# Norm chains ahead of weight parts, and sample products in larger steps, in a two-layer decoder step

## The chip, the cores and the metric

The kernel runs on one core of one Trainium2 chip. The metric is the device time of one execution in microseconds (us). An execution of the profiler gives the trace; the other times are without it. The engines are named as in the profile: PE (TensorE, the matrix products), PEld (its weight loads), DVE (VectorE), ACT (ScalarE), POOL (GpSimd), SP (SyncE, which here issues the loads).

## The reference

Two layers of a decoder trunk are computed for 256 prompt positions and 8 samples (one position each) that share the weights, 264 columns in all. Each layer adds four parts to x: half a SwiGLU feed-forward, a mixer (a short gated convolution in layer 0, the gated linear recurrence HGRN2 in layer 1), cross-attention to a memory, and half another SwiGLU.

```
def rmsnorm(x, g):
    y = xf * lax.rsqrt(jnp.mean(xf * xf, axis=-1, keepdims=True) + EPS)
    return (y * g.astype(jnp.float32)).astype(x.dtype)

def cross_attn(x, mk, mv, w_q, w_o):
    q = (x @ w_q).reshape(B, T, X_HEADS, X_HEAD_DIM)
    s = jnp.einsum('bthd,bnhd->bhtn', q, mk) / math.sqrt(X_HEAD_DIM)
    p = jax.nn.softmax(s, axis=-1)
    o = jnp.einsum('bhtn,bnhd->bthd', p, mv).reshape(B, T, D)
    return o @ w_o

        for i in range(DEPTH):
            h = rmsnorm(x, norm_ffn1[i])
            x = x + 0.5 * swiglu(h, w_ffn1_gate[i], w_ffn1_up[i], w_ffn1_down[i])
            h = rmsnorm(x, norm_mix[i])
            ...
            x = x + y
            h = rmsnorm(x, norm_xattn[i])
            x = x + cross_attn(h, mem_k[i], mem_v[i], w_xq[i], w_xo[i])
            h = rmsnorm(x, norm_ffn2[i])
            x = x + 0.5 * swiglu(h, w_ffn2_gate[i], w_ffn2_up[i], w_ffn2_down[i])
```

D is 1024, the feed-forward width 2816; attention has 4 heads of 256 and 256 memory positions, the recurrence 8 heads of 128. The prompt's memory keys and values are computed here (w_xkv, after a norm of the memory); the samples' keys and values (cache_mem_k, cache_mem_v, 8 MB each per layer) and the recurrence's states (8 x 8 matrices of 128 x 128) are read. All is float32.

## The kernel before, in words

**Products.** x stands transposed in memory: 8 tiles (KT) of 128 rows and 264 columns. Every float32 product of a projection is made of three fp32r products (mm3, L308 to L310): the high part of the activation times the high part of the weight, its low part times the weight's high part, and its high part times the weight's low part. kv (L847 to L849) does so with the memory as the stationary operand. Smaller things (transposes, scores, the samples' products) are plain f32 products, which leave two records each in the trace. Four PSUM banks take projections, four others ("aux") everything else.

**Weights.** Class Weights streams them in halves of 128 x 1024: SP loads raw, ACT casts it to wh (L107), DVE or, in attention's kv, POOL subtracts to wl (L119). Six buffers of raw, five of wh and wl.

**Norm chains.** A class Norm collects the squares of x, tile by tile, while the projection before it ends. Its finish() (L345 to L361) is a generator that runs beside the next projection: a cast nhi on ACT and nlo on DVE split the sums, two products with ones (ps_ms, L355 and L356) add over the rows, Ln and Exp on ACT (L288, helper rsqrt) and three Newton steps on DVE (L299, L303, L304) give R. The next projection runs on x without R; R enters where its banks are evicted (in attention qT, L833). So PE comes to wait for R only when it needs a fifth bank.

**What sets the order.** The program's lanes of generators (Flow) are advanced by a tick after every few products; each yield puts what follows one tick later. A scheduler then puts the instructions on the engines by that order and by priorities (tc.high_priority, offset HURRY), every engine runs its own in that order, and order() forbids it to put one instruction ahead of another on the same engine. One such bond exists: behind an out_proj the DVE parts wl stand behind the sum that frees a bank (L739).

**Attention.** mem_split (L819) makes mh and ml, eight high and low parts of the memory, on ACT and DVE. The query projection follows in four pieces; for each head sample_scores computes the samples' 64 dot products on DVE (L901) from a ring of four 1 MB slots. After it kv runs, head by head: its results become Kn and Vn (L857, ACT, then two output DMAs that ACT issues), transposed keys (pkt, L877; KTt), scores (psc, L929), softmax (mxp, Pp), transposed weights (ppt, L943; PTh, PTl) and values (po; oh, ol). The samples run beside: sample_rest takes maxima (mxs, transposed in pst, L976; top, tops, spread back by the product L980), exponentials, sums (L987), the weights Ps, and then the values spv (L1003), 128 rows from the ring by 8 columns, four heads side by side in 32 columns each; then os, spt and oh's sample columns (L1010 to L1018). Last comes the output projection.

**Recurrence.** samples() (L1237) multiplies the read states by the samples' queries (pqs, L1247), two heads and one ring slot at a time, in four columns of 32; head_norms (L1271) computes the norm of four heads (rr, rs), and gated (L1292) turns it into the output projection's input: prs (L1302), two products on DVE, then yh and yl, whose tiles are called kg and qf.

## Time and profile before

| | us |
|---|---|
| three runs, lowest / median / highest | 1303.28 / 1303.49 / 1303.51 |
| the profiled execution, whole | 1303.28 |
| its span, first to last instruction | 1301.3 |
| first attention: query projection's products | 301.6 to 327 |
| its kv, and its output projection | 327.2 to 393, 394.9 to 425 |
| recurrence: input projection, output projection | 809.3 to 942, 942.8 to 968 |
| second attention | 968.8 to 1091 |

The granted clock of PE was 0.997 of full speed. In the rows that follow, a line of the timeline gives start (us from the span's start), duration, engine, line of the kernel, operation, output <- inputs, shapes and count; brackets at its end tell how long the engine sat idle before it and for whom. "Duration" of a product includes its way through the array: back to back, products of one kind start 0.12 us apart (264 columns, fp32r) though each lasts 0.28. A row of the waits gives the engine, its line, whom it waited for, total us, times, and the longest.

### The profile page before, as it was taken

The numbers are of one execution on the slowest core, as the hardware profiler recorded it, in microseconds if no ns is written. First come the engines' busy times: TensorE is split into PE (matmuls) and PEld (weight loads), VectorE is DVE, ScalarE is ACT, GpSimd is POOL, SyncE is SP. The second block draws the span as 40 slices with busy tenths as digits, with TensorE's granted clock in tenths as the row PEclk, the third lists the DMA queues.
The fourth block names the chain that finished last, engine by engine and source line by source line (L and its number), as shares of the span: only waits on it lengthen the run. The fifth ranks groups of instructions, "written<-read, shape, count | busy, mean of one in ns | idle before, by whom it ended". The sixth has DMA issues, their size and how long they took to land.

```text
span 1301.3 us, 25953 instructions
## 1 busy us (share of the span) xinstructions
PE 1279.6 (98%) x10310; PEld 1236.4 (95%) x10310; DVE 824.1 (63%) x1570; ACT 694.5 (53%) x1146; POOL 293.5 (23%) x236
## 2 busy tenths in 40 slices
PE   8999999999999999999999999999999999999997
PEld 8999999999869999999999999999998779999996
DVE  6555567759826655556655545878789637766454
ACT  6454545446545645544554544656665447666542
POOL 3211231211741211132111132000023521211220
PEclk9999999999999999999999999999999999999998
DMA  8796555646997666556666556564557995776650
GB/s 269 245 302 178 166 182 175 208 142 201 357 379 218 195 180 178 185 164 201 179 178 186 176 175 186 157 195 136 169 157 257 394 327 160 223 215 198 204 167 34
DMA packets 263099, 266.75 MB, mean 205 GB/s; under 512 B 8697, under 2 KB 259577, under 8 KB 260930
## 3 DMA queue, kind: packets, MB, share of 16 engines
q1 hardware_dynamic: 257150, 259.78, 63.9%
q10 hardware_dynamic: 5828, 5.32, 1.2%
q8 instruction: 81, 1.33, 0.4%
q14 instruction: 40, 0.33, 0.1%
HBM read 255.00 MB, written 10.07 MB: 204 GB/s over the span
## 4 chain that ended last, share of the span: by engine, by line
PE 94%; DVE 3%; ACT 2%; issue 0%; DMA 0%; POOL 0%; DVEq 0%; SPq 0%; ACTq 0%; POOLq 0%
PE pj L308 20%; PE pj L309 19%; PE pj L310 19%; PE dn L308 7%; PE dn L310 7%; PE dn L309 7%; PE kv L847 2%; PE kv L849 2%; PE kv L848 2%; PE spv L1003 1%; PE psc L929 1%; PE pl L1163 1%; DVE wl L119 1%; PE pj L381 1%; DVE xl L332 1%; ACT wh L107 1%
## 5 line engine op out<-in xcount | busy, mean ns | idle before, releaser
L119 DVE TENSOR_TENSOR wl<-raw,wh 128x1024 fp32r<-128x1024 f32 (+1 forms) x347 | 426.6, 1234 | 248.8 <-ACT wh L107 238.0
L308 PE MATMUL pj<-xh,wh 128*128 128x264 f32 x1952 | 558.7, 286 | 2.3 <-DVE qT L833 2.3
L309 PE MATMUL pj<-xl,wh 128*128 128x264 f32 x1952 | 553.6, 284 | 0.0
L310 PE MATMUL pj<-xh,wl 128*128 128x264 f32 x1952 | 553.1, 283 | 0.0
L107 ACT CAST wh<-raw 128x1024 fp32r<-128x1024 f32 (+1 forms) x406 | 415.2, 1032 | 240.6 <-PE pj L309 108.3
L308 PEld LDWEIGHTS pj<-xh,wh 128*128 128x128 f32 x1952 | 367.8, 188 | 4.6 <-DVE qT L833 2.7
L309 PEld LDWEIGHTS pj<-xl,wh 128*128 128x128 f32 x1952 | 368.0, 189 | 0.0
L310 PEld LDWEIGHTS pj<-xh,wl 128*128 128x128 f32 x1952 | 366.2, 188 | 0.0
L308 PE MATMUL dn<-ah,wh 128*128 128x264 f32 x704 | 200.9, 285 | 0.0
L310 PE MATMUL dn<-ah,wl 128*128 128x264 f32 x704 | 200.0, 284 | 0.0
L309 PE MATMUL dn<-al,wh 128*128 128x264 f32 x704 | 199.4, 283 | 0.0
L119 POOL TENSOR_TENSOR wl<-raw,wh 128x1024 fp32r<-128x1024 f32 (+1 forms) x61 | 142.9, 2350 | 194.7 <-ACT wh L107 148.0
L703 POOL TENSOR_TENSOR al<-a,ah 128x264 fp32r<-128x264 f32 x88 | 90.1, 1026 | 415.6 <-ACT ah L702 415.5
L310 PEld LDWEIGHTS dn<-ah,wl 128*128 128x128 f32 x704 | 132.7, 188 | 0.0
L308 PEld LDWEIGHTS dn<-ah,wh 128*128 128x128 f32 x704 | 132.4, 188 | 0.2
L309 PEld LDWEIGHTS dn<-al,wh 128*128 128x128 f32 x704 | 132.5, 188 | 0.0
L288 ACT ACTIVATE g<-g 128x264 f32<-128x264 f32 x88 | 36.9, 424 | 78.9 <-DVE g L695 78.8
L702 ACT CAST ah<-a 128x264 fp32r<-128x264 f32 x88 | 36.0, 413 | 65.1 <-DVE a L701 64.3
L330 ACT ACTIVATE xh<-xT,gains 128x264 fp32r<-128x264 f32 x56 | 28.7, 513 | 75.9 <-DVE xT L729 59.2
L901 DVE CUSTOM_DVE_ANT_0 junk<-ring,pq 128x256 f32<-128x256 f32 x128 | 53.7, 420 | 3.7
L701 DVE TENSOR_TENSOR a<-g,pj 128x264 f32<-128x264 f32 x88 | 37.1, 426 | 29.0 <-PE pj L310 28.9
L695 DVE TENSOR_TENSOR g<-pj,R_norm_ffn 128x264 f32<-128x264 f32 x88 | 37.5, 429 | 28.1 <-PE pj L310 28.0
(329 smaller groups left out, 1494.3 us busy)
## 6 DMA issues: line engine op xcount, KB each, us to landing
raw<-in_w_ffn_gate_dram SPq DMA_DIRECT2D x88, 512.0 KB, 5.2
raw<-in_w_ffn_up_dram SPq DMA_DIRECT2D x88, 512.0 KB, 4.1
raw<-in_w_ffn_down_dram SPq DMA_DIRECT2D x64, 512.0 KB, 4.2
ring<-in_cache_mem_k_dram SPq DMA_DIRECT2D x16, 1024.0 KB, 6.6
raw<-in_w_xkv_dram SPq DMA_DIRECT2D x64, 256.0 KB, 3.6
ring<-in_cache_mem_v_dram SPq DMA_DIRECT2D x16, 1024.0 KB
raw<-in_w_rec_in_dram SPq DMA_DIRECT2D x32, 512.0 KB, 4.4
raw<-in_w_ffn_down_dram SPq DMA_DIRECT2D x32, 384.0 KB, 3.0
```

What stands on the lines that cost most here:

```text
L107: self.pin(copy(wh[:, :n], self.raw[i][:, :n]))
L119: ins = eng.tensor_sub(wl[:, :n], self.raw.pop(i)[:, :n], wh[:, :n].bitcast(F32))
L288: in_line(nc.scalar.activation(dst, src, func, **kw))
L308: nc.tensor.matmul(ps, wh[:, s], rh, start=first, stop=False)
L309: nc.tensor.matmul(ps, wh[:, s], rl, start=False, stop=False)
L310: nc.tensor.matmul(ps, wl[:, s], rh, start=False, stop=last)
L330: pin(nc.scalar.activation(h, src, AF.Copy, scale=g))
L695: nc.vector.tensor_mul(g, ps, norm.R)
L701: nc.vector.tensor_mul(a, g, ps)
L702: nc.scalar.copy(ah[:, blk], a)
L703: nc.gpsimd.tensor_sub(al[:, blk], a, ah[:, blk].bitcast(F32))
L901: nc.vector.tensor_tensor_reduce(junk, t[:, i % 8], pq[:, :XD], 1.0, 0.0, ALU.mult, ALU.add, sc[:, h, i : i + 1])
```

## The change

It does five things.

1. finish() of every norm loses one yield before the sums of squares, and Ln, Exp and the Newton steps get the priority HURRY. The last Exp and the last Newton step are noted in W.after; every later wh on ACT, wl on DVE, and the parts mh and ml are bound to stand behind them.
2. mem_split starts when the norm is done instead of after six ticks.
3. tops, the spread maxima, has 128 rows (zero below the fourth), and so has the product that uses it.
4. The values yield after two ring slots instead of one, and give both back together.
5. The recurrence's samples take four heads and two slots in one step, with one bank for its transposes and sums; the head norms and the gated products get HURRY and the same bond as in 1.

```diff
-        self.pin(copy(wh[:, :n], self.raw[i][:, :n]))
+        self.pin(self.behind(self.hi[i % len(self.hi)], copy(wh[:, :n], self.raw[i][:, :n])))
...
+    def behind(self, eng, ins):
+
+        if eng in self.after:
+            self.order(ins, self.after[eng], "products in line")
+        return ins
...
             yield
-            yield
             ps = aux_bank("ps_ms")
             nc.tensor.matmul(ps[:, :NC], ones_d, hi, start=True, stop=False)
             nc.tensor.matmul(ps[:, :NC], ones_d, lo, start=False, stop=True)
-            rsqrt(self.R, ps[:, :NC])
-            if self.after is not None:
-                use_set(self.after)
-            newton(self.R, ps[:, :NC], self.acc)
+            with tc.high_priority(offset=HURRY):
+                rsqrt(self.R, ps[:, :NC])
+                W.after["s"] = last[0]
+                if self.after is not None:
+                    use_set(self.after)
+                W.after["v"] = newton(self.R, ps[:, :NC], self.acc).ins
             self.done = True
...
             def mem_split():
-                for _ in range(6):
+                while not norm.done:
                     yield
                 for k in range(KT):
                     g = gcol("norm_mem", l, k)
-                    nc.scalar.activation(mh[:, k], memT[:, k], AF.Copy, scale=g)
...
+                    W.behind("s", nc.scalar.activation(mh[:, k], memT[:, k], AF.Copy, scale=g))
...
-                nc.tensor.matmul(pt[:, P : P + XH], tops, ident[:XH, :XH], start=True, stop=True)
+                nc.tensor.matmul(pt[:, P : P + XH], tops, ident[:, :XH], start=True, stop=True)
...
-                    if i % 2 == 1:
-                        ring.done((l, "v", i // 2))
+                    if i % 4 == 3:
+                        for i2 in (i // 2 - 1, i // 2):
+                            ring.done((l, "v", i2))
                         yield
...
             def samples(a):
 
                 s = gr[a]
-                for p in (2 * a, 2 * a + 1):
-                    hs = slice(2 * p, 2 * p + 2)
+                hs = slice(GH * a, GH * a + GH)
+                ps = aux_bank("pqs")
+                for p2 in range(2):
+                    p = 2 * a + p2
                     S0 = ring.tiles["s", p].rearrange("p (h b v) -> p h b v", h=2, b=NB)
-                    ps = aux_bank("pqs")
                     for j in range(4):
                         for c in range(4):
                             hh, hf = divmod(c, 2)
                             nc.tensor.matmul(
-                                ps[32 * c : 32 * c + 4, :P],
+                                ps[32 * c : 32 * c + 4, p2 * P : p2 * P + P],
...
-                    for c in range(4):
-                        nc.scalar.copy(os[32 * c : 32 * c + 4], ps[32 * c : 32 * c + 4, :P])
...
+                for c in range(4):
+                    nc.scalar.copy(os[32 * c : 32 * c + 4], ps[32 * c : 32 * c + 4, : 2 * P])
...
+                pd = pt[:, 2 * P : 2 * P + GH * NB]
+                nc.tensor.matmul(pd, ones_1, qk.rearrange("p a b -> p (a b)"), start=True, stop=True)
...
-                rsqrt(rr, pm[:, :NC])
-                use_set(SIGMOID)
-                newton(rr, pm[:, :NC], tmp)
-                nc.scalar.copy(rs, rr)
-                nc.vector.scalar_tensor_tensor(rs, rs.bitcast(F32), seconds_of, rr, op0=ALU.mult, op1=ALU.add)
+                with tc.high_priority(offset=HURRY):
+                    rsqrt(rr, pm[:, :NC])
+                    W.after["s"] = last[0]
+                    newton(rr, pm[:, :NC], tmp)
+                    nc.scalar.copy(rs, rr)
+                    use_set(SIGMOID)
+                    W.after["v"] = nc.vector.scalar_tensor_tensor(
+                        rs, rs.bitcast(F32), seconds_of, rr, op0=ALU.mult, op1=ALU.add
+                    ).ins
```

The three places at which the order matters most follow; names end in the scheduler's tile numbers, which differ between the two programs, and the new file's lines are 7 to 20 higher.

DVE in layer 0, from the split of the sum of squares (nlo) to the first evictions of the query projection (qT). Before:

```order
L351 TENSOR_TENSOR nlo<-nacc_norm_xattn_2596,nhi 128x264
L825 SCALAR_TENSOR_TENSOR ml<-memT,gains,mh 128x256 x8
L119 TENSOR_TENSOR wl_3905<-raw_3677,wh_3891 128x1024
L119 TENSOR_TENSOR wl_3932<-raw_3699,wh_3907 128x1024
L299 SCALAR_TENSOR_TENSOR nacc_norm_xattn_2596<-ps_ms,R_norm_xattn_2597 128x264
L303 SCALAR_TENSOR_TENSOR nacc_norm_xattn_2596<-nacc_norm_xattn_2596,R_norm_xattn_2597 128x264
L304 SCALAR_TENSOR_TENSOR R_norm_xattn_2597<-nacc_norm_xattn_2596,R_norm_xattn_2597 128x264
L833 TENSOR_TENSOR qT_3963<-pj_0_3825,R_norm_xattn_2597 128x264
L833 TENSOR_TENSOR qT_3963<-pj_1_3826,R_norm_xattn_2597 128x264
L833 TENSOR_TENSOR qT_3966<-pj_0_3827,R_norm_xattn_2597 128x264
```

After:

```order
L358 TENSOR_TENSOR nlo<-nacc_norm_xattn_2596,nhi 128x264
L306 SCALAR_TENSOR_TENSOR nacc_norm_xattn_2596<-ps_ms,R_norm_xattn_2597 128x264
L310 SCALAR_TENSOR_TENSOR nacc_norm_xattn_2596<-nacc_norm_xattn_2596,R_norm_xattn_2597 128x264
L311 SCALAR_TENSOR_TENSOR R_norm_xattn_2597<-nacc_norm_xattn_2596,R_norm_xattn_2597 128x264
L120 TENSOR_TENSOR wl_3915<-raw_3677,wh_3893 128x1024
L836 SCALAR_TENSOR_TENSOR ml<-memT,gains,mh 128x256
L120 TENSOR_TENSOR wl_3936<-raw_3699,wh_3917 128x1024
L845 TENSOR_TENSOR qT_3969<-pj_0_3827,R_norm_xattn_2597 128x264
L845 TENSOR_TENSOR qT_3969<-pj_1_3828,R_norm_xattn_2597 128x264
L845 TENSOR_TENSOR qT_3972<-pj_0_3829,R_norm_xattn_2597 128x264
L845 TENSOR_TENSOR qT_3972<-pj_1_3830,R_norm_xattn_2597 128x264
L836 SCALAR_TENSOR_TENSOR ml<-memT,gains,mh 128x256 x3
```

The three Newton steps (L306, L310, L311) now follow nlo at once; the eight ml, which stood ahead of them, are spread from there into the dot products, and two wl slid behind R.

ACT in layer 1, at the second head norm of the recurrence: from the table load ahead of Ln and Exp (rr) to the casts kg of the output projection's input. Before:

```order
L284 ACT_TABLE_LOAD
L288 ACTIVATE rr<-pm,eps_t 128x264
L107 CAST wh_11541<-raw_11209 128x1024
L288 ACTIVATE rr<-rr 128x264
L284 ACT_TABLE_LOAD
L107 CAST wh_11567<-raw_11241 128x1024
L288 ACTIVATE q<-G 128x264
L284 ACT_TABLE_LOAD
L1287 CAST rs<-rr 128x264
L107 CAST wh_11623<-raw_11331 128x1024
L107 CAST wh_11639<-raw_11375 128x1024
L1308 CAST kg<-oT 128x264 x4
```

After:

```order
L291 ACT_TABLE_LOAD
L295 ACTIVATE rr<-pm,eps_t 128x264
L295 ACTIVATE rr<-rr 128x264
L291 ACT_TABLE_LOAD
L295 ACTIVATE q<-G 128x264
L107 CAST wh_11516<-raw_11184 128x1024
L1303 CAST rs<-rr 128x264
L107 CAST wh_11542<-raw_11216 128x1024
L291 ACT_TABLE_LOAD
L1328 CAST kg<-oT 128x264
```

Ln and Exp stand side by side, two wh no longer stand between Ln and q, one follows q instead; a table load and a wh lie between rs and the first kg, where two wh stood.

PE in layer 0, at the end of kv. Before, the rows behind the last values (spv), and, after more kv products and the values po of head 2, the first rows of the output projection (pj of oh):

```order
L847 MATMUL kv_1_4721<-wh_4611,mh 128x512
L848 MATMUL kv_1_4721<-wl_4629,mh 128x512
L849 MATMUL kv_1_4721<-wh_4611,ml 128x512
L1014 MATMUL spt<-ident,os 128x128 x2
L943 MATMUL ppt<-ident,Pp 128x128 x4
L847 MATMUL kv_0_4720<-wh_4658,mh 128x512
```

```order
L308 MATMUL po<-PTh,Vh_4684 128x256
L309 MATMUL po<-PTl,Vh_4684 128x256
L310 MATMUL po<-PTh,Vl_4685 128x256
L308 MATMUL pj_0_4894<-oh,wh_4690 128x264
L309 MATMUL pj_0_4894<-ol,wh_4690 128x264
```

After, the rows behind the last values, up to the output projection's first:

```order
L1014 MATMUL spv<-ring_4642,Ps 8x256 x8
L860 MATMUL kv_0_4758<-wl_4733,mh 128x512
L861 MATMUL kv_0_4758<-wh_4691,ml 128x512
L859 MATMUL kv_1_4759<-wh_4691,mh 128x512
L860 MATMUL kv_1_4759<-wl_4733,mh 128x512
L861 MATMUL kv_1_4759<-wh_4691,ml 128x512
L1026 MATMUL spt<-ident,os 128x128 x2
L889 MATMUL pkt<-ident,Kn_4721 128x128 x4
L315 MATMUL pj_0_4895<-oh,wh_4735 128x264
L315 MATMUL pj_1_4896<-oh,wh_4735 128x264
L941 MATMUL psc<-KTt_4780,qT_4018 128x256 x4
L316 MATMUL pj_0_4895<-ol,wh_4735 128x264
```

The last values moved to five products ahead of kv's end; head 2's transposes (pkt, L889), scores (psc, L941) and all that follows now stand between or behind the first products of the output projection, which before had twelve po products ahead of it.

More of the change, by code (lines that the diff above doesn't have):

```diff
@@ L66, in __init__ @@
         self.pin = lambda ins: ins
-        self.behind = lambda ins: None
+        self.order, self.after = None, {}
     def add(self, *srcs):
@@ L274, in order @@
         tc.add_manual_dep(ins.ins, first.name, info, reason=reason)
+    W.order = order
     def in_line(ins):
@@ L303, in newton @@
         nc.vector.scalar_tensor_tensor(tmp, tmp, -0.5, dst, op0=ALU.mult, op1=ALU.mult)
[L304 removed]
+        return nc.vector.scalar_tensor_tensor(dst if out is None else out, tmp, 1.5, dst, op0=ALU.add, op1=ALU.mult)
     def mm3(ps, w, rh, rl, first, last, s=slice(None)):
@@ L404, in project @@
             W.release()
-            W.behind = lambda ins: None
             if need is not None:
@@ L738, in evac @@
             if k == KT - 1:
-                W.behind = lambda ins: order(ins, add.ins, "the sum that frees a bank")
+                W.after["v"] = add.ins
             nxt.kt(k)
@@ L817, in attention @@
             nc.gpsimd.memset(os, 0.0)
+            tops = ap.tile([P, P], F32, name="tops")
+            nc.gpsimd.memset(tops, 0.0)
             def mem_split():
-                for _ in range(6):
+                while not norm.done:
                     yield
@@ L971, in sample_rest @@
                 top = ap.tile([XH, NB], F32, name="top")
-                tops = ap.tile([XH, P], F32, name="tops")
                 nc.vector.reduce_max(mx, sc, axis=AX.X)
@@ L1035, in rec @@
             qfz = rp.tile([P, RH, 2, 16], F32, name="qfz")
-            os = rp.tile([P, P], F32, name="os")
+            os = rp.tile([P, 2 * P], F32, name="os")
             nc.gpsimd.memset(os, 0.0)
@@ L1253, in samples @@
                             )
-                    ring.done(("s", p))
-                    for c in range(4):
-                        nc.scalar.copy(os[32 * c : 32 * c + 4], ps[32 * c : 32 * c + 4, :P])
-                    qk = tl("qk", 2, (P, 2, NB))
-                    nc.vector.tensor_mul(qk, qs[:, hs], ks[:, hs])
-                    yield
-                    pt = aux_bank("pqt")
-                    nc.tensor.transpose(pt[:, :P], os, ident)
-                    pd = aux_bank("pd")[:, : 2 * NB]
-                    nc.tensor.matmul(pd, ones_1, qk.rearrange("p a b -> p (a b)"), start=True, stop=True)
-                    nc.vector.tensor_mul(oT[:, hs, T:], vs[:, hs], pd.rearrange("p (h b) -> p h b", h=2))
-                    dst = oT[:, hs, T:].rearrange("p h (f j) -> p h f j", f=2)
-                    ptv = pt[:, :P].rearrange("p (h f r) -> p h f r", h=2, f=2)[:, :, :, :4]
-                    nc.vector.tensor_add(dst, dst, ptv)
-                    yield
+                for p2 in range(2):
+                    ring.done(("s", 2 * a + p2))
+                for c in range(4):
+                    nc.scalar.copy(os[32 * c : 32 * c + 4], ps[32 * c : 32 * c + 4, : 2 * P])
+                qk = tl("qk", 1, (P, GH, NB))
+                nc.vector.tensor_mul(qk, qs[:, hs], ks[:, hs])
+                yield
+                pt = aux_bank("pqt")
+                for p2 in range(2):
+                    nc.tensor.transpose(pt[:, p2 * P : p2 * P + P], os[:, p2 * P : p2 * P + P], ident)
+                pd = pt[:, 2 * P : 2 * P + GH * NB]
+                nc.tensor.matmul(pd, ones_1, qk.rearrange("p a b -> p (a b)"), start=True, stop=True)
+                nc.vector.tensor_mul(oT[:, hs, T:], vs[:, hs], pd.rearrange("p (h b) -> p h b", h=GH))
+                dst = oT[:, hs, T:].rearrange("p h (f j) -> p h f j", f=2)
+                ptv = pt[:, : 2 * P].rearrange("p (h f r) -> p h f r", h=GH, f=2)[:, :, :, :4]
+                nc.vector.tensor_add(dst, dst, ptv)
+                yield
                 s["old"] = True
```

26 lines of the change are left out of this document (14 added, 12 removed).

## The prediction

> **What bounds the kernel now.** I read the page first (busy time by engine, then the chain of waits), then the table of PE's waits, then the timelines around each wait.
>
> ```profile
> PE 1279.6 (98%) x10310; PEld 1236.4 (95%) x10310; DVE 824.1 (63%) x1570; ACT 694.5 (53%) x1146; POOL 293.5 (23%) x236
> PE 94%; DVE 3%; ACT 2%; issue 0%; DMA 0%; POOL 0%; DVEq 0%; SPq 0%; ACTq 0%; POOLq 0%
> ```
>
> TensorE (PE) is the bound: busy 98% of the span, and 94% of the chain that ended last. The change alters almost none of its products, so only two things can move the time: microseconds in which PE stands, and what it pays to change from one kind of product to another. The table of PE's waits lists the first; its columns are total us, times, longest.
>
> ```profile
> PE pj L308 <- DVE qT L833: 2.3, 2, 1.2
> PE po L308 <- ACT PTh L949: 1.3, 2, 0.7
> PE pj L308 <- ACT oh L965: 1.3, 2, 0.7
> PE pj L308 <- ACT kg L1308: 1.3, 1, 1.3
> PE pst L980 <- DVE tops L978: 0.4, 2, 0.2
> ```
>
> Rows one and four are in reach of the change: 2.3 us at the query projections of both layers, 1.3 us at the output projection of the recurrence. Rows two and three are the last prompt head of each attention; its instructions keep their order, so they stay. No row names an evicted bank of a feed-forward part (g) or the conv part, so the norm chains of those stages hold PE up nowhere today.
>
> **A. Norm chain of attention (gain 2.35).** PE, DVE and ACT of layer 0:
>
> ```profile
> 309.04 0.28 PE L355 MATMUL ps_ms<-nhi,ones_d 128*128 128x264 f32 x1
> ...
> 313.40 0.29 PE L309 MATMUL pj<-xl,wh 128*128 128x264 f32 x1
> 313.53 0.28 PE L310 MATMUL pj<-xh,wl 128*128 128x264 f32 x1
> 315.04 0.39 PE L308 MATMUL pj<-xh,wh 128*128 128x264 f32 x1 [1.23 <-DVE qT L833]
> ...
> 307.30 0.42 DVE L351 TENSOR_TENSOR nlo<-nacc_norm_xattn,nhi 128x264 fp32r<-128x264 f32 x1
> 307.64 3.25 DVE L825 SCALAR_TENSOR_TENSOR ml<-memT,gains,mh 128x256 fp32r<-128x256 f32 x8
> 310.81 2.35 DVE L119 TENSOR_TENSOR wl<-raw,wh 128x1024 fp32r<-128x1024 f32 x2
> 313.08 0.43 DVE L299 SCALAR_TENSOR_TENSOR nacc_norm_xattn<-ps_ms,R_norm_xattn 128x264 f32<-128x264 f32 x1
> 314.55 1.46 DVE L833 TENSOR_TENSOR qT<-pj,R_norm_xattn 128x264 f32<-128x264 f32 x4
> ...
> 306.65 2.51 ACT L824 ACTIVATE mh<-memT,gains 128x256 fp32r<-128x256 f32 x6
> 309.06 1.99 ACT L107 CAST wh<-raw 128x1024 fp32r<-128x1024 f32 x2
> 310.95 0.47 ACT L288 ACTIVATE R_norm_xattn<-ps_ms,eps_t 128x264 f32<-128x264 f32 x1
> 311.45 0.42 ACT L288 ACTIVATE R_norm_xattn<-R_norm_xattn 128x264 f32<-128x264 f32 x1
> ```
>
> The starts of PE's last two rows are 1.51 us apart, those before them 0.13 (0.12 on the mean of a stretch): 1.39 us lost, 1.23 of it idle and 0.16 to start again. By the table's 2.3 the other layer idled about 1.1, so lost about 1.25. The bank's eviction (qT) waits for R, and R is late because eight mh and two wh stand ahead of its Ln on ACT, and eight ml and two wl ahead of its Newton steps on DVE. In the new order only one wh stands between nhi and Ln, and nothing between nlo and the Newton steps. nlo still ends at 307.72; two sums of squares, Ln and Exp (0.9) and three Newton steps (0.43 each) put R at about 310.4, four microseconds earlier. What is late next is DVE: one wl, one ml and one wl (1.2 + 0.4 + 1.2) now follow R and end about 313.2, the first qT about 313.6, when PE arrives at 313.53. I leave 0.15 per layer: 1.39 + 1.25 - 0.3 = 2.35.
>
> Seven of the eight ml (3.25/8 = 0.41 each) move behind R, into the stretch of sample scores in which DVE has next to no idle time, and PE comes 1.4 us sooner. The scores thus end almost 3 us later against PE. The new order answers this: the first transpose of the sample maxima stands 13 kv products later, 13 x 0.23 = 3.0 us. Cover about equal to delay; what is left goes into E.
>
> **B. Head norms of the recurrence (gain 1.65).**
>
> ```profile
> 949.34 0.28 PE L310 MATMUL pj<-kg,wl 128*128 128x264 f32 x1
> 950.94 0.76 PE L308 MATMUL pj<-kg,wh 128*128 128x264 f32 x4 [1.33 <-ACT kg L1308]
> ...
> 944.64 1.06 ACT L107 CAST wh<-raw 128x1024 fp32r<-128x1024 f32 x1
> 945.59 0.42 ACT L288 ACTIVATE q<-G 128x264 f32<-128x264 f32 x1
> 946.03 1.28 ACT L284 ACT_TABLE_LOAD   x1
> 947.33 0.41 ACT L1287 CAST rs<-rr 128x264 fp32r<-128x264 f32 x1
> ```
>
> 950.94 - 949.34 - 0.12 = 1.48 us lost. Between the first rr and the cast of rs, ACT had two wh and two table loads; in the new order it has one of each, so rs comes 1.06 + 1.28 = 2.3 us sooner, at about 945.0. The products prs move up by 18 products (18 x 0.12 = 2.2 us), so they still fit. The table load does not vanish: with one wh it stands between rs and the first kg, which can start at 945.0 + 0.41 + 1.06 + 1.28 = 947.8, where PE wants it at 949.5. I count the whole 1.48 as gone, and 0.17 for the smaller stall at prs itself; the margin is some 1.3 us after the cast.
>
> **C. Recurrent samples, four heads at a time (gain 0.8).**
>
> ```profile
> 850.35 0.28 PE L310 MATMUL pj<-xh,wl 128*128 128x264 f32 x1
> 850.55 1.06 PE L1247 MATMUL pqs<-ring,qfz 128*4 128x128 f32 x32
> 851.54 0.39 PE L308 MATMUL pj<-xh,wh 128*128 128x264 f32 x1
> 851.77 0.29 PE L309 MATMUL pj<-xl,wh 128*128 128x264 f32 x1
> ```
>
> One run costs 851.77 - 850.35 = 1.42 us, less two ordinary steps of 0.12 and eight sets at (1.06 - 0.27)/7 = 0.11: 0.30 for going in and out. The order shows two runs in place of four: 0.6. The ones-products pd halve (four records, by an estimate 0.05 each): 0.2. The copies on ACT and DVE halve too, beside PE, worth nothing.
>
> **D. Start of the attention's output projection (cost 1.5 per layer).** The values were to run for two slots at a time, but the order has eight runs per layer as before (two of the first slot's pieces are new, two neighbours merged), so they save nothing. What moves is their surroundings: the last run stands later, the products that covered its consumers are now ahead of it, and head 2 of the prompt has slid behind it.
>
> ```profile
> 388.51 1.49 ACT L1010 COPY os<-spv 8x256 f32<-8x256 f32 x4 [1.30 <-PE spv L1003]
> 390.10 1.05 ACT L107 CAST wh<-raw 128x1024 fp32r<-128x1024 f32 x1
> 391.18 0.21 ACT L1017 CAST oh<-spt 128x64 fp32r<-128x64 f32 x1
> ...
> 389.40 0.39 PE L848 MATMUL kv<-wl,mh 128*128 128x512 f32 x1
> 389.63 0.40 PE L849 MATMUL kv<-wh,ml 128*128 128x512 f32 x1
> 390.05 0.44 PE L1014 MATMUL spt<-ident,os 128*128 128x128 f32 x2
> ...
> 399.74 1.89 PE L929 MATMUL psc<-KTt,qT 128*128 128x256 f32 x8
> ...
> 401.67 0.69 DVE L913 TENSOR_REDUCE mxp<-psc 128x2 f32<-128x512 f32 x1 [2.22 <-PE psc L929]
> ```
>
> Before, six kv products lay between the last values and spt (389.63 to 390.05 is 0.42 where 0.23 is usual: 0.19 stall), and oh (391.39) was not wanted until twelve products of head 2 later. Now five lie there: 0.23 + 0.19 = 0.42 stall. After spt and four transposes (0.7) PE wants oh, which has os, wh and the cast ahead of it: it comes at 391.4 where PE arrives at 390.75, 0.68 stall. Then two products, and psc of head 2 waits for KTt: 0.1. psc ends some 1.7 later; mxp, the exponentials and their scaling follow on DVE and ACT, behind four copies of Kn and Vn and two issues of output DMAs that are queued on ACT. That chain takes about 2.7 us, and 21 products (2.5) cover it: 0.2. The transposed weights of head 2 meet a cover of six products (0.7) for two casts of 0.6 and 0.7: 0.1. More changes between f32 and fp32r products, 0.2. Sum 1.7, less the 0.19 that is there now: 1.5, in two layers 3.0. Ends: nothing, if everything on DVE and ACT comes a little sooner; 3.4 per layer if head 2 is exposed as the last head is (rival 3).
>
> **E. Start of the values (0.3 per layer, 0.6).** New splits of the first slot, the remainder of A's delay, and the fourth slot's transfer, which is issued only when the scores free its slot: between 0 and 1.0 per layer. Later transfers (two slots released together) have some five microseconds of margin and cost nothing.
>
> **F. Sums of squares 12 products sooner (0.3).** All seven norms issue them 12 x 0.12 = 1.46 us earlier: in A's rows at 309.04 - 1.46 = 307.58, where nlo ends at 307.72, 0.14 behind. The other attention and one feed-forward norm are as close, the rest have over 1 us.
>
> **G. Maxima on 128 rows (nothing).**
>
> ```profile
> L980 PE MATMUL pst<-ident,tops x4: 248/258/268, 358.3 to 1025.3; 4*128 4x4 f32 x4
> L987 PE MATMUL pst<-zss,peers x4: 169/211/253, 360.7 to 1027.6; 128*128 128x4 f32 x4
> ```
>
> Per tile, min/median/max ns: the products with 4 rows took 258, the next ones with 128 rows 211, two per layer. That is at most 0.1 to 0.2 us per layer, and the tops that they wait for (0.4 in the waits) come no sooner: I count zero, with 0.3 below it for the range. The Trainium skill, "TensorE: Matmul & The Clock Gate", says in its summary table that a small-K matmul takes the same time alone as one of K=128, by which more rows win nothing; "TensorEngine Tiling (Array Packing)", Key Properties, says that changing the tiling mode drains the engine, by which 128 rows would save a change. The rows lean to the second; by it the sum would be some 0.3 lower.
>
> **Sum.** Against the profiled execution's 1303.28 (span 1301.3 and 2.0 around it; the median of the three runs is 1303.49, 0.2 above): gains 2.35 + 1.65 + 0.8 = 4.8, costs 3.0 + 0.6 + 0.3 = 3.9; 1303.28 - 0.9 = **1302.4**.
>
> **Rivals.**
> 1. **The new waits are covered.** If the order's new places are right, D is nothing and only E and F remain: 1303.3 - 4.8 + 0.9 = 1299.4. For it: DVE is 63% busy, and after 357 us mostly free; against it: oh's three ACT instructions in a row, which nothing shortens. Chance 0.32.
> 2. **The attention norm's wait stays**, since wl, ml and wl between R and qT are held up by ACT, where wh and eight mh (2.51/6 = 0.42 each) follow Exp. Then A gives nothing: 1304.7. For it: the first ml needs the first mh, and the second wl the second wh; against: both are early in that queue. Chance 0.10.
> 3. **Head 2 becomes a second last head (slower).** The table shows that an uncovered head costs 1.3/2 + 1.3/2 us in PTh and oh, and more in PTl and restarts, about 2.3 per layer; with the 1.1 for spt and oh that is 3.4 in place of 1.5: 1302.4 + 2 x 1.9 = 1306.2. It decides where the exponentials of head 2 on ACT start over 2 us behind psc, as they would when the copies of Kn and Vn or the issue of the output DMAs fall just there. Chance 0.18.
>
> The forecast itself has 0.40.
>
> **Numbers.** About 0.2% (2.6 us) is what a measurement of this kernel tells from no change, so faster means below 1300.9, slower above 1306.1. Faster: rival 1 and a little of the forecast's spread, 0.35. Slower: rival 3 and a little, 0.20. Same: 0.45. The range runs from just under rival 1 to just over rival 3, 1299.0 to 1306.4; it takes in C and G fully paid and E at its far end.
>
> **What would show it.** The wait for qT gone from PE's table, or below 0.4 in all (A); no kg row (B); two runs of 64 pqs records (C); new rows for spt and for oh from L1029 of the new file, 0.4 and 0.7 per layer (D); psc of head 2 late by little. Rival 1 shows no such rows, rival 3 has PTh at twice its 1.3. The forecast is wrong if a transfer of a ring slot appears in PE's waits, or if the feed-forward norms, which I hold at nothing, turn up there.

## The result, and the profile after

The changed kernel takes **1309.79 us** (median of 6 runs, 1307.43 to 1310.71) where the kernel before takes 1303.5 (6 runs, 1303.28 to 1304.41): ratio 1.0042, interval 1.0032 to 1.0052. It is slower by about 6 us; the forecast of 1302.4 and its range to 1306.4 were both too low. The profiled execution took 1310.22 us, its span 1308.4. The granted clock of each run is on record: 0.997 and 0.998 in the two lowest of the six, 0.995 or 0.996 in the other four.

From the page of the changed kernel, the busy time of PE and the chain that ended last; from the table of PE's waits (total us, times, longest) the rows that are new or clearly up:

```profile
PE 1283.5 (98%) x10306; PEld 1239.3 (95%) x10306; DVE 824.2 (63%) x1564; ACT 694.1 (53%) x1138; POOL 294.5 (23%) x238
PE 96%; DVE 2%; ACT 1%; DMA 0%; issue 0%; SPq 0%; DVEq 0%; ACTq 0%
```

```profile
PE ppt L955 <- DVE Pp L933: 4.2, 3, 2.0
PE pj L389 <- DVE wh L107: 1.5, 1, 1.5
PE pj L315 <- ACT oh L1029: 0.9, 2, 0.4
PE spt L1026 <- ACT os L1022: 0.5, 2, 0.3
```

The rows for qT (2.3) and for kg (1.3) are gone, as forecast. The rows for spt and oh of the samples are there, as forecast. The first row is not in the prediction at all: PE waits 2.0 us in each layer for the transposes of head 0's weights (ppt), that is for their scaling on DVE (Pp); the third wait in this row is below 0.2. PE's busy time has also grown by 3.9 us: part of it is products that ran slower.

The table gives, stage by stage, what PE lost (+) or gained (-) against the kernel before: the start of the first product of the next stage, minus the same in the kernel before, minus what it was when the stage began. All come from PE's timelines, counted from PE's first product, and the profiled runs of the experiments below are in it too.

| kernel | start | query projection, layers 0 and 1 | memory's products to end of attention's output projection, layers 0 and 1 | recurrence: input, output projection |
|---|---|---|---|---|
| changed | +1.2 | -1.35, -1.39 | +4.60, +6.24 | -1.28, -1.52 |
| e1 | +1.4 | -1.34, -1.40 | +3.22, +3.62 | -1.26, -1.55 |
| e2 | +0.9 | 0, 0 | +4.39, +6.08 | 0, 0 |
| e3 | +0.1 | -1.39, -1.38 | +3.11, +3.32 | -1.29, -1.52 |
| e4 | +0.4 | 0, 0 | -0.09, +0.15 | 0, 0 |
| e5 | +1.7 | -1.37, -1.28 | +3.16, +3.22 | 0, 0 |
| e6 | +0.1 | -1.36, -1.39 | +1.57, +1.60 | -1.28, -1.51 |
| e7 | +0.1 | -1.38, -1.40 | +0.80, +3.45 | -1.22, -1.57 |
| e8 | -0.1 | 0, 0 | +0.24, 0 | -1.21, -1.54 |
| e9 | 0 | -1.39, -1.38 | +3.37, +3.34 | -1.26, -1.52 |
| e10 | -0.1 | -1.41, -1.39 | +1.13, +1.21 | -1.26, -1.55 |
| e11 | +1.5 | -0.05, +0.41 | -0.09, 0 | -1.25, -1.56 |

So the gains came, and were even larger than forecast: 2.74 + 1.28 + 1.52 = 5.5 us. What came with them in the third column is 10.8 us, where the forecast had 3.6 (D and E). The column "start" is the first feed-forward projection; in its first 16 us, where the difference arises, the order of instructions is the same in the kernel before and the changed one, so it moves by itself (see the last section).

**What happens at head 0.** Timelines of DVE, POOL and PE in layer 0, first of the kernel before, then of the changed one (start, us, engine, line, operation):

```profile
348.32 0.62 DVE L921 TENSOR_SCALAR Pp<-Pp,zsp 128x256 f32<-128x256 f32 x2
348.82 4.78 POOL L119 TENSOR_TENSOR wl<-raw,wh 128x1024 fp32r<-128x1024 f32 x2 [2.16 <-ACT wh L107]
```

```profile
348.30 0.35 DVE L933 TENSOR_SCALAR Pp<-Pp,zsp 128x256 f32<-128x256 f32 x1
348.57 0.41 DVE L913 CUSTOM_DVE_ANT_0 junk<-ring,pq 128x256 f32<-128x256 f32 x1
348.90 2.39 DVE L933 TENSOR_SCALAR Pp<-Pp,zsp 128x256 f32<-128x256 f32 x1
...
348.79 4.77 POOL L120 TENSOR_TENSOR wl<-raw,wh 128x1024 fp32r<-128x1024 f32 x2 [2.15 <-ACT wh L107]
...
349.07 0.27 PE L955 MATMUL ppt<-ident,Pp 128*128 128x128 f32 x1
351.35 0.55 PE L955 MATMUL ppt<-ident,Pp 128*128 128x128 f32 x3 [2.01 <-DVE Pp L933]
```

Before, the two scalings (one per 128 positions) run back to back, 0.62 together, and have nearly ended when POOL begins its two subtractions of 4.77 / 2 = 2.39 each. In the changed kernel a dot product of the sample scores stands between them; that the seven moved ml bring this order is what e11 shows. The second scaling starts 0.11 us after POOL's subtraction and takes 2.39 us instead of 0.35: it ends at 351.29, when POOL's first one (half of the 4.77) has just ended. The dot product that follows beside POOL's second one takes its 0.41 as ever. The four transposes of a head leave one record each, so the x1 and the x3 are all of head 0. In layer 1 the same happens:

```profile
1016.21 2.38 DVE L933 TENSOR_SCALAR Pp<-Pp,zsp 128x256 f32<-128x256 f32 x1
```

The profile of the kernel before had such a hold already, where nothing waits for it. Its sixteen scalings, min/median/max ns:

```profile
L921 DVE TENSOR_SCALAR Pp<-Pp,zsp x16: 340/351/1473, 348.3 to 1071.8; 128x256 f32<-128x256 f32 x16
```

The longest runs from 364.98 to 366.45, under a subtraction of POOL from 363.90 to 366.30. PE's waits have no row for Pp there, so it cost nothing; but one row of a constant form with a maximum of four times its median was the warning.

**What follows in layer 1.** The view of stretches (length, busy time of PE, PEld, DVE, ACT, POOL, then the granted TensorE clock, DMA share and GB/s):

```profile
1016.00:1018.90 2.90, 0.89 (x6) 0.50 (x5) 2.90 (x5) 1.06 (x2) 2.81 (x2) 0.99 1.03 395
1018.90:1022.00 3.10, 3.10 (x10) 2.52 (x9) 2.93 (x14) 0.59 (x1) 1.93 (x1) 0.50 1.06 367
```

After the stall the clock is at 0.50 for 3.4 us, and seven kv products take 0.43 instead of 0.23 each: 7 x 0.2 = 1.4 us more. Layer 0 has the same stall and keeps 1.00 (the last section says what differs); the difference of the two layers in the table, 6.24 - 4.60 = 1.6, is about this.

**Start of the output projection.** PE and ACT of layer 0:

```profile
393.73 0.44 PE L1026 MATMUL spt<-ident,os 128*128 128x128 f32 x2 [0.26 <-ACT os L1022]
394.00 0.60 PE L889 MATMUL pkt<-ident,Kn 128*128 128x128 f32 x4
395.04 0.51 PE L315 MATMUL pj<-oh,wh 128*128 128x264 f32 x2 [0.43 <-ACT oh L1029]
...
392.18 1.49 ACT L1022 COPY os<-spv 8x256 f32<-8x256 f32 x4 [1.53 <-PE spv L1014]
393.70 1.05 ACT L107 CAST wh<-raw 128x1024 fp32r<-128x1024 f32 x1
394.77 0.21 ACT L1029 CAST oh<-spt 128x64 fp32r<-128x64 f32 x1
```

This is term D as it was worked out: spt waits for os, and oh stands behind a wh on ACT.

### The profile page after: what moved, and what is told of

Read it like the earlier page. It is cut to its first block, busy times and chain, and to the rows that moved or that the text cites. A ratio compares the mean times of both kernels' runs of the same rounds, so it can differ in the third digit from the quotient of the medians.

```text
span 1308.4 us, 25931 instructions
## 1 busy us (share of the span) xinstructions
PE 1283.5 (98%) x10306; PEld 1239.3 (95%) x10306; DVE 824.2 (63%) x1564; ACT 694.1 (53%) x1138; POOL 294.5 (23%) x238
## 4 chain that ended last, share of the span: by engine, by line
PE 96%; DVE 2%; ACT 1%; DMA 0%; issue 0%; SPq 0%; DVEq 0%; ACTq 0%
PE pj L315 21%; PE pj L316 20%; PE pj L317 20%; PE dn L315 7%; PE dn L317 7%; PE dn L316 6%; PE kv L861 2%; PE kv L859 2%; PE kv L860 2%; PE spv L1014 1%; PE psc L941 1%; PE pl L1175 1%; PE pj L389 1%; DVE Pp L933 0%; DMA raw<-in_w_ffn_gate_dram 0%; PE ppt L955 0%
```

## The experiments

Theory 1: the loss is mainly a DVE instruction held for as long as the GpSimd subtraction that runs at that moment, and it came within reach because the displaced ml split the pair of scalings. Rivals: the values' two slots cause it; the weight parts' new bonds cause it; the two engines merely slow one another; the loss only appears when all parts come together.

**e1: the scalings on ScalarE.** The changed kernel with one line other, for all four heads of the prompt:

```
-  nc.vector.tensor_scalar(pr[:, r], pr[:, r], zs[:, r : r + 1], None, op0=ALU.mult)
+  nc.scalar.activation(pr[:, r], pr[:, r], AF.Copy, scale=zs[:, r : r + 1])
```

> The changed kernel with one edit: the scaling of the prompt's softmax weights (Pp, two instructions per head) is done by ACT instead of DVE; all else stays, but for a few rows around head 2. Theory 1 (shared port): in the changed kernel the second scaling of head 0 starts on DVE just behind the start of a weight subtraction on POOL and is held until that ends (2.39 us instead of 0.35); on ACT nothing holds it. Then PE's 2.0 us wait for ppt of head 0 goes in both layers (at most 0.3 left each), the stretch of half clock behind it in layer 1 goes too, and the time falls by 4.3 us and more: about 1303, from 1307.4 to 1310.5. Theory 2 (DVE is late because seven ml moved into its dense stretch): the maxima and reciprocals are still made by DVE at the same times, so ppt of head 0 still waits 1 us or more per layer, and the time stays within 1.5 us of 1307.4.

1304.57 us (11 runs, 1304.34 to 1309.8), ratio 1.0011, interval 1.0002 to 1.002. The wait for Pp is gone. The first of these rows has come up from 0.7, the other two stay:

```profile
PE po L316 <- DVE PTl L962: 1.5, 2, 0.8
PE pj L315 <- ACT oh L1029: 0.9, 2, 0.4
PE spt L1026 <- ACT os L1022: 0.5, 2, 0.3
```

Three microseconds come back (1307.4 to 1304.3 between the lowest runs), not the 4.3 that were expected: ACT needs 0.91 for the two scalings and makes the parts that follow late, and the rest of the column (3.2 in layer 0) lies elsewhere.

**e2: the kernel before, its pair of scalings split.** A reduction of 0.69 us, whose result nothing uses, stands between the two scalings of head 0:

```
+  if h == 0 and r == 0:
+      extra = ap.tile([P, rows], F32, name="extra")
+      between = nc.vector.reduce_max(extra, src, axis=AX.X)
+      order(between, ins.ins, "a reduction between")
...
```

> The kernel before, with one reduction over the scores of head 0 (0.69 us, its result unused, reads PSUM) put on DVE between the two scalings of head 0 in each layer. It moves the second scaling from about 348.6 to 349.2, which is behind the start of POOL's subtraction (348.8 to 351.2); the scheduler then moves three of the four transposes ppt two kv products back. Theory 1 (shared port): the second scaling takes about 2.0 us and ends when POOL's subtraction does; PE waits 1.3 to 1.7 us for ppt in each layer; with some 0.8 per layer for values that the new order splits, the time is 1306 to 1309. Theory 2: the scaling takes 0.35 us, PE does not wait for ppt, and the time is at most 1305.5 (the splits alone).

1314.91 us (4 runs, 1314.15 to 1315.05), ratio 1.0085, interval 1.0071 to 1.0099: more than expected. DVE, POOL and PE's waits:

```profile
350.14 2.14 DVE L922 TENSOR_SCALAR Pp<-Pp,zsp 128x256 f32<-128x256 f32 x1
361.16 2.00 DVE L985 COPY tops<-top 4x128 f32<-4x128 f32 x1
...
349.76 4.77 POOL L119 TENSOR_TENSOR wl<-raw,wh 128x1024 fp32r<-128x1024 f32 x2 [2.15 <-ACT wh L107]
358.37 4.71 POOL L119 TENSOR_TENSOR wl<-raw,wh 128x1024 fp32r<-128x1024 f32 x2 [3.84 <-ACT wh L107]
...
PE pst L987 <- DVE tops L985: 3.5, 2, 1.7
PE ppt L950 <- DVE Pp L922: 3.1, 2, 1.6
```

One instruction of 0.69 us in the kernel before is enough to bring the loss of the changed one. The shift that it makes brings a second instruction under POOL: the copy of the maxima (tops), 0.65 before, takes 2.00 and ends at 363.16, as POOL's second subtraction of that pair does (358.37 + 4.71 = 363.08). This second hold was not expected (3.5 us of waits); two half-clock stretches in the profiled run, at the start (+0.9) and in layer 1 behind the second hold, make up most of the rest of the miss.

**e3: the changed kernel with the values one slot at a time.**

```
-  if i % 4 == 3:
-      for i2 in (i // 2 - 1, i // 2):
-          ring.done((l, "v", i2))
+  if i % 2 == 1:
+      ring.done((l, "v", i // 2))
```

> The changed kernel, but the values yield and give their slot back after each ring slot, as before. Head 2's transposes and scores return into kv. Theory: the cost of the start of the output projection (spt 0.4, oh 0.6 to 0.7 in each layer, and small products wedged between its own) comes from this part of the change alone, so about 1 to 2 us per layer go: 1.5 to 4 us below the changed kernel run beside it; the 2.4 us scaling on DVE and the wait for ppt of head 0 stay, 2.0 us per layer. Rival: the place of spt and oh follows from the norm part (DVE's delay): then the waits for spt and oh stay and the time is within 1 us of the changed kernel.

1304.3 us (10 runs, 1304.03 to 1306.04), ratio 1.0008, interval 0.9999 to 1.0017. The rows for spt and oh are gone, the one for Pp stays:

```profile
PE ppt L955 <- DVE Pp L933: 4.2, 2, 2.2
```

The values' two slots cost 4.60 - 3.11 = 1.5 us in layer 0, which is term D; they are not the cause of the hold.

**e4: the kernel before with the values two slots at a time** (the same edit the other way).

> The kernel before with this part alone: the values yield after two ring slots and give two back together. The order has seven runs of values per layer instead of eight, unsplit, and head 2's transposes behind spt as in the changed kernel, though still inside kv. Theory: one run less saves 0.3 per layer; the new waits (spt 0.2 more, head 2's chain in the output projection, products wedged in) cost 0.5 to 1.5 per layer: the time is 1303.5 to 1306. No wait for ppt of head 0, no long scaling. Rival: the costs in the output projection need DVE's delay by the norm part; then this is 0.5 below the kernel before.

1303.46 us (10 runs, 1303.18 to 1304.53), ratio 1.0001, interval 0.9992 to 1.001: no difference, and no row for spt or oh in PE's waits. So what cost 1.5 in layer 0 of the changed kernel costs nothing alone. That it costs only where the values come late against PE fits (in e7, where nothing is held in layer 0, they start 2.5 us later after the first kv product than before), but no run tests this by itself.

**e5: the kernel before with the norm part alone** (R's chain in a hurry, weight parts and memory split behind it, sums of squares sooner):

```
+  with tc.high_priority(offset=HURRY):
+      rsqrt(self.R, ps[:, :NC])
+      W.after["s"] = last[0]
...
+      W.after["v"] = newton(self.R, ps[:, :NC], self.acc).ins
...
-  for _ in range(6):
+  while not norm.done:
       yield
```

> The kernel before with the norm part alone: R's chain in a hurry, weight parts and the split of the memory bound behind it, sums of squares 12 products sooner. Values, maxima and the recurrence stay as before. Theory 1 (a scaling held by the subtraction on GpSimd): the seven displaced ml put a dot product between the two scalings of head 0's weights, as in the changed kernel, so the wait for Pp of head 0 stands in PE's table with about 4.2 us for 2, while the wait for qT is gone (gain 2.7): 1303.5 - 2.7 + 4.3 + some 1.5 for new splits = about 1306.5 (1305 to 1308). Rival (the wait comes from the values' two slots, or only from all parts together): no wait for Pp, and about 1301 to 1302. A half clock behind the stall would add up to 1.5 to either.

1309.58 us (4 runs, 1307.18 to 1310.42), ratio 1.0042, interval 1.0029 to 1.0054. Theory 1 expected 1305 to 1308, and the mechanism that it names is there; the median lies above. In the profiled run, 1308.82, the start takes 1.7 us of it, with a half-clock stretch.

```profile
PE ppt L953 <- DVE Pp L931: 4.0, 2, 2.0
```

The norm part alone gains its 2.65 and loses 3.16 + 3.22 = 6.4, of which about 2 per layer are the hold and about 1 is something else. It stands where the changed kernel stands: there the recurrence's gain of 2.8 and the cost of the values' two slots, 3.0, come on top and cancel.

**e6: both repairs, e1 and e3 together.**

> The changed kernel with both repairs: head 0's scalings on ScalarE, and the values one slot at a time. Theory 1 (the loss is the sum of two things that do not depend on one another, the held scaling of 4.3 us and the values' rearrangement of about 3 us): the changed kernel without its clock events is at 1307.4, so 1307.4 - 3.0 - 3.1 = about 1301.3 with ScalarE's longer scalings still in the way, 1299 to 1302; no wait for Pp, spt or oh over 0.3 in PE's table. Rival (the two overlap, since what waits for the one would be late for the other anyway): about 1304, as each repair gives alone.

1301.86 us (12 runs, 1300.95 to 1306.81), ratio 0.9992, interval 0.9982 to 1.0001. The profiled run took 1301.05, as the sum of the two repairs says; the two do not overlap. Four of the twelve runs lie at 1303.9 to 1306.8, with a granted clock of 0.995 to 0.997 on record where the six lowest have 0.998; they have no trace, so where the clock fell stays open.

**e7: scalings side by side on VectorE, values one slot at a time.** The changed kernel with e3's edit and:

```
+  with tc.high_priority(offset=HURRY):
       nc.vector.reciprocal(zs, zs)
       for r in range(rows):
           nc.vector.tensor_scalar(pr[:, r], pr[:, r], zs[:, r : r + 1], None, op0=ALU.mult)
```

> The changed kernel with the reciprocal and the scalings in a hurry on VectorE, so that both scalings of head 0 stand side by side as in the kernel before, and the values one slot at a time. Theory 1: both scalings of head 0 take some 0.35 us each if they start ahead of GpSimd's subtraction, the wait for Pp is gone, and the time is 1303.5 - 5.5 (attention norm 2.7, four heads 1.3, head norms 1.5) + 1 to 2 for splits = 1299 to 1300. Rival (the delay and not the order decides: the dot products are late, so the scalings start behind GpSimd's subtraction all the same): a scaling of over 2 us remains, about 1303 to 1304. If side by side helps as much as ScalarE does, it also shows that the engine that scales is no cause by itself.

**1299.85 us** (7 runs, 1299.39 to 1302.15), ratio 0.9975, interval 0.9964 to 0.9985: faster than both kernels. No wait for Pp. The profiled run took 1302.15 and shows in layer 1 another instruction held, the split of V (DVE, POOL, PE):

```profile
1017.98 2.84 DVE L877 TENSOR_TENSOR Vl<-Vn,Vh 128x512 fp32r<-128x512 f32 x1
...
1017.87 7.52 POOL L120 TENSOR_TENSOR wl<-raw,wh 128x1024 fp32r<-128x1024 f32 x3 [1.91 <-ACT wh L107]
...
1023.80 0.27 PE L988 MATMUL pst<-ident,mxs 128*4 128x128 f32 x1 [1.74 <-DVE mxs L985]
```

Again 0.11 us decide: POOL starts at 1017.87, DVE at 1017.98. The split ends near 1020.8, the dots behind it are late, and the maxima of the samples come 1.7 us late. In layer 0 nothing is held, and the stage costs only 0.80.

**e8: the kernel before with the recurrence part alone** (samples four heads at a time, head norms and gated rows in a hurry, weight parts behind them; its edits are those of the diff in that function).

> The kernel before with the recurrence part alone: samples for four heads at a time, head norms and gated rows in a hurry, weight parts bound behind them. Theory 1 (these parts are independent of the attention's): the input projection gains 1.3 and the output projection of the recurrence 1.5, no wait for kg, two runs of 64 sample products: 1303.5 - 2.8 = 1300.7 (1300.2 to 1301.2). Rival (part of the gain seen in the changed kernel is shifted from the attention's stage, or given back in the next one): 1302 to 1303.5.

1300.84 us (10 runs, 1300.63 to 1302.47), ratio 0.998, interval 0.9971 to 0.9989, as theory 1 said. These parts give 2.75 in the recurrence's stages and take at most 0.24 in one attention. The attention norm's wait is unchanged:

```profile
PE pj L315 <- DVE qT L839: 2.3, 2, 1.2
```

**e9: the changed kernel, each subtraction on GpSimd in four quarters.** The order of every other engine stays the same, row for row:

```
-  ins = eng.tensor_sub(wl[:, :n], self.raw.pop(i)[:, :n], wh[:, :n].bitcast(F32))
-  self.pin(self.behind(lo, ins))
+  raw, step = self.raw.pop(i), 1 if lo == "p" else n
+  for k in range(0, n, step):
+      ks = slice(k, k + step)
+      self.pin(self.behind(lo, eng.tensor_sub(wl[:, ks], raw[:, ks], wh[:, ks].bitcast(F32))))
```

> The changed kernel with each subtraction on GpSimd written as four of 128x256 in place of one of 128x1024; the order of every other engine is the same, row for row. Theory 1 (the scaling of head 0's weights on VectorE is held until the GpSimd instruction that runs at that moment ends): a quarter ends after some 0.6 us, so the longest scaling falls from 2.39 to at most about 1.0, the wait for Pp from 4.2 us to 1.5 or less, and the half clock of the second layer goes: about 1304.5 (1303.5 to 1305.5) where the changed kernel has 1307.4 to 1310.7. Rival (the two engines share a path and both run slower while they overlap, or the scaling waits for something else): four quarters overlap as much as one whole does, the longest scaling stays above 2 us and the time at 1307 to 1310.

1305.21 us (11 runs, 1304.96 to 1305.44), ratio 1.0011, interval 1.0002 to 1.0021. DVE and POOL at head 0 of both layers, and PE's wait:

```profile
347.11 0.35 DVE L935 TENSOR_SCALAR Pp<-Pp,zsp 128x256 f32<-128x256 f32 x1
347.71 0.77 DVE L935 TENSOR_SCALAR Pp<-Pp,zsp 128x256 f32<-128x256 f32 x1
...
1013.80 0.77 DVE L935 TENSOR_SCALAR Pp<-Pp,zsp 128x256 f32<-128x256 f32 x1
...
347.60 5.66 POOL L123 TENSOR_TENSOR wl<-raw,wh 128x256 fp32r<-128x256 f32 x8 [1.46 <-ACT wh L107]
...
PE ppt L957 <- DVE Pp L935: 1.4, 4, 0.5
```

The second scaling starts 0.11 us after POOL as before, and now takes 0.77 in place of 2.39: it waits for a quarter, not for a whole. Had the two engines merely slowed one another on a path that they share, eight quarters in a row would have slowed it as much as two wholes. This is the run that names GpSimd's instruction as what holds DVE. It also takes the half clock of layer 1 away (+3.34 beside +3.37). The quarters are no remedy by themselves: POOL's 1024 columns now take 4 x 0.79 = 3.1 us in place of 2.35 on the mean; and the trace shows that POOL is held in turn: the quarter at 567.47, which started 0.33 us behind a subtraction of DVE, took 1.73 where the median quarter takes 0.74.

**e10: e7 with the quarters.**

> The kernel of e7 (scalings side by side, values one slot at a time) with the subtractions on GpSimd in quarters. There, in the second layer, the split of V on VectorE ran 2.84 us beside GpSimd's subtraction, and the first transpose of the sample maxima waited 1.7 us, the second 0.8. Theory 1: that split falls to 1.3 us or less, the wait for mxs to below 0.5, and the time from 1299.85 to about 1298.5 (1297.8 to 1299.4), with less spread between runs. Rival (GpSimd in quarters is slower as a whole, or the wait for mxs has another cause): 1299.4 to 1300.5, the wait for mxs still 1.5 or more.

1300.74 us (11 runs, 1300.52 to 1301.55), ratio 0.9977, interval 0.9968 to 0.9986: theory 1 expected 1298.5, and the wait for mxs is indeed gone, but the time is no better than e7's. The stage costs 1.13 and 1.21 where e7 had 0.80 in the layer without a hold, and 0.5 us more than before lie behind PE's last product. Quarters remove this hold, and the kernel gains nothing by them.

**e11: the changed kernel with the memory's split where it was, and the values one slot at a time.**

```
-  while not norm.done:
+  for _ in range(6):
       yield
...
-      W.behind("s", nc.scalar.activation(mh[:, k], memT[:, k], AF.Copy, scale=g))
+      nc.scalar.activation(mh[:, k], memT[:, k], AF.Copy, scale=g)
```

(and the same for ml).

> The changed kernel with the split of the memory at its old place and unbound (eight mh and ml ahead of R's chain again) and the values one slot at a time; R's chain still in a hurry with the weight parts behind it. On VectorE both scalings of head 0 then stand side by side again, with no other edit to them. Theory 1 (the displaced ml delay the dot products and so split the pair; the attention norm's gain and the loss hang on the same move): no wait for Pp, but the wait for qT is back with about 2 us for 2, since two wl still stand between R and the first eviction; of the change the recurrence's 2.8 remain: about 1300.7 (1300.2 to 1301.5). Rival (binding the weight parts and the sums of squares 12 products sooner cost something by themselves, or delay the scores as well): 1303 or more. A third way (Ln needs only one wh less, and the chain is early enough): the wait for qT falls to half, about 1299.5.

1301.84 us (10 runs, 1300.68 to 1302.22), ratio 0.998, interval 0.9971 to 0.999; four runs lie at 1300.7 to 1301.2, six at 1301.7 to 1302.2, the profiled one among these with +1.5 at the start. Against e3 only the memory's split (mh and ml) has moved, and the wait for Pp is gone while this one is back:

```profile
PE pj L315 <- DVE qT L842: 2.6, 2, 1.5
```

The third column falls to -0.09 and 0. So the attention norm's gain and the whole loss hang on the same move, as theory 1 said; the weight parts' bonds and the earlier sums of squares cost 0.4 at most.

## Why the prediction was wrong

**The step that failed** is the end of A: "Cover about equal to delay; what is left goes into E." It priced the 2.9 us that seven ml take from DVE by one consumer, the first transpose of the sample maxima, and found it covered. It never asked what else DVE does in the stretch into which the ml move. There the scalings of prompt head 0 are interleaved with the dots, and there POOL starts a subtraction just as the pair ends. The second scaling was held 2.0 us too long, and PE waited 2.0 us per layer for it: e2 brings such a wait (1.6 per layer) into the kernel before, e9 bounds it by a quarter, e11 takes it away. In layer 1 the clock fell to 0.50 after the wait, another 1.4. No rival held this mechanism; rival 3 ended on the right side, 1306.2, for another reason, and did not occur: the wait for PTh is 1.5 in the changed kernel and was 1.3.

The Trainium skill, "SBUF — State Buffer", section "SBUF: two separate sides", says that VectorE and GpSimd share a pair of ports as an exclusive lock: whichever of GpSimd's instruction and a VectorE instruction in a two-port mode or with two SBUF inputs starts first has it for the whole instruction, and the other is blocked. The trace agrees: 2.39 us in wholes, 0.77 in quarters, and a dot product with one input in PSUM not slowed at all (0.41).

Point by point:

- **A, wait for qT**: right and better than forecast. 2.74 against 2.35; the row is gone. R's last Newton step ends at 311.9, and the first qT starts behind the two wl at 314.4 without PE waiting (1.3 of these times is the later start; without it R ends at 310.5, where 310.4 was forecast):

```profile
311.43 0.43 DVE L311 SCALAR_TENSOR_TENSOR R_norm_xattn<-nacc_norm_xattn,R_norm_xattn 128x264 f32<-128x264 f32 x1
314.44 1.45 DVE L845 TENSOR_TENSOR qT<-pj,R_norm_xattn 128x264 f32<-128x264 f32 x4
```

- **B, head norms**: 1.52 against 1.65, right; e8 shows it alone, 1.54.
- **C, four heads at a time**: 1.2 to 1.3 against 0.8, right in kind, the size too small.
- **D, start of the output projection**: 1.5 per layer, the size right (e3), and the rows for spt (0.3) and oh (0.4) where they were expected, a little shorter. Its cause was put down incompletely: the values' order costs nothing in the kernel before (e4), so it takes the rest of the change besides; that A's delay of the values is what it takes is likely, and not shown.
- **E, start of the values**: mis-sized. 0.3 was forecast; e3 leaves 3.11 - 2.15 = 1.0 per layer when the hold is taken off, and e7 and e10, without any hold in layer 0, 0.8 and 1.1. PE's steps of e7 in layer 0 show what it is made of: the values still have eight runs, but the first 48 records come in pieces of 4, 2 and 42 that take 3.79 us where three runs of 16 took 2.94, +0.85; the other steps of the stage (+0.3 at the scores, -0.4 at kv) about cancel. The far end of E's bounds, 1.0, was the right value.
- **F**: too small to be seen by itself. e11, which keeps the earlier sums of squares, has -0.05 and +0.41 at the query projections, the second with a longer wait for qT; in the feed-forward stages behind the start no kernel moves by more than 0.1.
- **G, maxima on 128 rows**: zero, right. Min/median/max ns of the tops products in the changed kernel, where they were 248/258/268:

```profile
L991 PE MATMUL pst<-ident,tops x4: 253/263/273, 362.7 to 1031.7; 128*128 128x4 f32 x4
```

  So the rule of "TensorE: Matmul & The Clock Gate" in the Trainium skill (few rows take the same time alone as 128) fits, and the rule by which 128 rows would save a change of tiling mode has nothing to show for it here. The forecast had seen a lean to the second rule in 258 against 211 ns; that was a difference between two products, not between 4 and 128 rows.

The sum, with what was measured for a run without clock events: gains 2.74 + 1.28 + 1.52 = 5.5; costs 4.3 (hold) + 3.0 (D) + 2.0 (E) = 9.3; 1303.4 + 3.8 = 1307.2, where the lowest runs lie at 1307.4. In the profiled run the half clock of layer 1 and the start add 1.4 and 1.2: 1309.8, where it took 1310.22.

What remains open: what exactly makes D cost in the changed kernel alone, and where the clock fell in four runs of e6.

## What to carry to other kernels

When instructions are moved on one engine, list everything that this engine does in the stretch that receives them, not only the chain that one had in mind, and look there for neighbours whose order will change. Where VectorE and GpSimd both work from SBUF, a VectorE instruction on the critical path should start clear of GpSimd's, or be kept next to its twin; a tenth of a microsecond decides over the whole length of GpSimd's instruction. A gain that was measured together with a loss is best taken apart: keep the recurrence's parts (2.75 us), and the attention's norm part only with the scalings in a hurry and the values one slot at a time, 1299.85 in all. That last step is worth 1.0 us over e8's 1300.84, and the two intervals overlap.

## What the runs showed of the hardware that was not expected

A stall of 2.0 us was enough to bring TensorE's granted clock to 0.50 for 3.4 us, in layer 1 of the changed kernel but not in layer 0; e3 and e5 have stalls of 2.0 to 2.2 us in both layers and keep 1.00. The clock records of the traces show what differs. The changes of the clock lie on a grid: in the changed kernel at 11.89, 15.30, 1018.82 and 1022.24, that is 3.41 us apart, and 1018.82 - 15.30 = 294 x 3.413. On this grid the whole stall of layer 1 falls into one step, 1015.41 to 1018.82, with 2.01 us idle, and the next step is at half clock; layer 0's is cut at 349.80 into 0.46 and 1.55. The most idle steps of e3 and e5 in the attention have 1.71 and 1.54, with no half clock behind them; a step of e2 with 1.73, 1031.79 to 1035.20, has one. So in these traces the idle time within one step decides, and not the length of the stall alone.

The like happens at the very start, where DVE's cast of the second weight part lies under POOL's first subtraction and PE waits for it: the kernel before waited 0.7 us there and had the first of these stretches, the changed one waited 1.5 and had the second, 1.2 us longer in all:

```profile
12.00:14.00 2.00, 1.92 (x14) 1.83 (x15) 2.00 (x6) 2.00 (x4) 2.00 (x2) 1.00 1.09 385
```

```profile
12.00:14.00 2.00, 2.00 (x10) 1.74 (x10) 2.00 (x7) 2.00 (x4) 2.00 (x2) 0.50 1.09 385
```

The profiled runs of e1, e2, e5 and e11 have it too (+0.9 to +1.7). Less idle time was enough there: 1.24 us in a step brought it in e1, 1.23 did not in e4, and why it takes less than in the attention stays open. That the kernel before has runs near 1303.4 and near 1304.5 fits: the granted clock on record is 0.997 or 0.998 in the former and, but for one, 0.996 in the latter. With the subtractions in quarters the wait is 0.4 in e9, and its eleven runs lie within 0.5 us. The Trainium skill, "TensorE: Matmul & The Clock Gate", section on the clock gate (Part 1), lets the clock fall after an idle window of about 3.4 us; here 1.2 to 2.0 us without products went ahead of it, so the measurement speaks for a window in which not all is idle.
